# Tracing the four sink heads ahead of the query projection, and storing gates 6 to 8 before their sigmoid

## Chip, cores and metric

One core of one Trainium2 chip. The metric is device time in microseconds (us) from launch to the end of the program, as a median over runs. A core has TensorE (PE), VectorE (DVE), ScalarE (ACT), GpSimd (POOL) and SyncE (SP, which here only issues DMAs). Each works through its own list of instructions, and semaphores hold an instruction back until what it needs is there.

## The reference, cut to what matters

Two layers; each is a half-step feed-forward, a mixing block, and another half-step feed-forward. The mixing block projects the normed input once and feeds three kinds of attention, whose outputs are merged under sigmoid gates:

```python
h = rms_norm(x, mix_norm[l])
(nq, nkc, nvc, nks, nvs, nkw, nvw, ngate, sq, sk, sv, wq, wk, wv, bgate) = jnp.split(h @ w_in[l], SPLIT_POINTS, axis=-1)
y_nsa = nsa_attention(...)            # 8 heads, queries nq, RMS-normed per head
y_sb  = stick_breaking_attention(...) # 4 heads
y_swa = swa_sink_attention(...)       # 4 heads, window 128, a sink logit in the softmax
g = sigmoid(bgate).reshape(B, S, 3, D_MODEL)
merged = g[:, :, 0] * (y_nsa @ w_up_nsa[l]) + g[:, :, 1] * (y_sb @ w_up_sb[l]) + g[:, :, 2] * (y_swa @ w_up_swa[l])
x = x + merged @ w_out[l]
```

The sequence has 512 positions, D_MODEL is 1024, a head is 64 wide. All is float32; the kernel forms a float32 product as three matmuls of a high and a low part.

## The kernel before, in words

Positions lie in four tiles of 128 (`NT`), the model width in eight tiles (`KD`). The order of instructions on each engine is made when the program is built: the code is traced in the order in which it is written, each tile takes a buffer of its pool in that order, and a scheduler then places each instruction on its engine's list when its own model of the engines says that it can start. So the code's order decides who gets a buffer first, and the scheduler decides who stands before whom.

PSUM has eight banks, each of them one buffer (`b0` to `b7`). `psum(...)` says which banks the tiles of a name take in turn. The next tile of a bank can't be written before the last reader of the one before it.

`mix_front` makes everything that comes ahead of the 8 NSA heads: six projections (`project`, L670), head norms, transposes, the stick-breaking heads, the compressed keys and values, and the four heads with sinks (`sliding`). Between them it computes gates ahead. There are 24 gate tiles (3 branches by 8 columns). Gates 0 to 8 (`EARLY = 9`) come by `gate_early` in `mix_front`: 24 matmuls each (L204 to L206, output `g`, weights split by `pieces` into `ghi` on ACT at L195 and `glo` on DVE at L196), a multiplication on DVE (L1092), a sigmoid on ACT (L1075) and a store to DRAM (`gkept`, L1076). Gates 9 to 23 are computed while the NSA heads run and get their sigmoid in `mix_back` (L1201).

One head of `sliding` takes four score tiles (L863, two matmuls of 128x256 each, output `s`), reads each of them on DVE with the bias added and the row's bound found (L865), takes the exponential on ACT (`exp`, L816), divides on POOL (L876), transposes (L879 to L887) and multiplies by the values. `exp` puts each exponential behind all sigmoids traced up to there (`behind`, an order on ACT without a semaphore), so that ACT changes its table once, at the first exponential.

Before the change the end of `mix_front` runs: compressed keys and values; `project(l, 5)`, the queries of NSA; gate 6; `evacuate` (L689) and `head_norms` of the queries (L701 and L702 the sums, L351 to L356 the root, L707 the scaling on DVE, L709 the weights on POOL); their transposes; gates 7 and 8; then `sliding` with score banks 0 and 1. The gates have banks 6 and 2.

Of the kernel before, what the change touches and what calls it, by code (L numbers as in the profile page):

```python
# [12 lines left out]
AF = mybir.ActivationFunctionType  # L13
# [38 lines left out]

EARLY = 9
MORE = (2, 1, 1, 1, 1, 1, 2)

COMPRESS = ((), (0, 1), (2,), (3,))

# [37 lines left out]
def trunk(ctx, tc, I, out):  # L95
    nc = tc.nc
    pe, act, dve, pool, sp = nc.tensor, nc.scalar, nc.vector, nc.gpsimd, nc.sync
# [9 lines left out]
    def nm(s):  # L107
        cnt[0] += 1
        return f"{s}_{cnt[0]}"
# [19 lines left out]
    def psum(**sets):  # L129

        turn.clear()
        for tag, ids in sets.items():
            turn[tag] = itertools.cycle(ids)

    def bank(tag):
        i = next(turn[tag])
        return ps.tile([P, S], F32, name=nm(tag), tag=f"b{i}")
# [541 lines left out]
    def heads(ap, n):  # L679
        return ap.rearrange("p (h d) -> p h d", h=n)  # L680
# [129 lines left out]
    sigmoids = {}  # L810
# [131 lines left out]
    def compress_out(l, p, which):  # L942

        pre = unit("cp")[0:DH]
        act.copy(pre, p[0:DH, 0:CW])
        dve.tensor_tensor(pre, pre, p[DH:P, 0:CW], op=ALU.add)
        hid = unit("cp")[0:DH]
        sigmoids[which] = act.activation(hid, pre, AF.Sigmoid)
        dve.tensor_tensor(hid, hid, pre, op=ALU.mult)
        pb = bank("f")  # L950
        for c in range(2):
            pe.transpose(pb[:, c * DH : (c + 1) * DH], hid[:, c * P : (c + 1) * P], ident[0:DH, 0:DH])
        hT = unit("cp")[:, 0:P]
        dve.tensor_copy(hT, pb[:, 0:P])
        w2 = sm.tile([P, 2, DH], F32, name=nm("w2"), tag="w2", bufs=1)
        sp.dma_start(w2, I[f"w2{which}"][l])
        p = bank("f")
        for g in range(2):
            for c in range(2):
                pe.matmul(p[0:32, g * DH : (g + 1) * DH], hT[:, c * DH + g * 32 : c * DH + g * 32 + 32], w2[:, c], start=c == 0, stop=c == 1)  # L960
        return p[0:32, 0:P]
# [26 lines left out]
    def compressed_v(p):  # L988
        vc = sm.tile([64, 2, 2, DH], F32R, name=nm("vc"), tag="vc", bufs=1)
        for r in (0, 32):  # L990
            act.copy(vc[r : r + 32, :, 0], heads(p, 2))
        for r in (0, 32):
            dve.tensor_tensor(vc[r : r + 32, :, 1], heads(p, 2), f32(vc[0:32, :, 0]), op=ALU.subtract)
        return vc
# [77 lines left out]

    def gate_early(l, i, nrm, between=lambda: None):
        g = gate_logits(l, i, nrm, "gs", between)
        sigmoids["early"] = act.activation(g, g, AF.Sigmoid)  # L1075
        sp.dma_start(gkept[i], g)  # L1076

    def gate_logits(l, i, nrm, tag, between=lambda: None):
# [35 lines left out]
    def mix_front(l, nrm, more):  # L1114
        rows = sm.tile([P, 6, DH], F32, name=nm("rows"), tag="rows", bufs=1)
        sp.dma_start(rows, I["hnorms"][l : l + 1].rearrange("a b c -> a (b c)").to_broadcast([P, 6 * DH]).rearrange("p (b c) -> p b c", b=6))
        sinks = sm.tile([P, 2 * SWH], F32, name=nm("sinks"), tag="sinks", bufs=1)
        sp.dma_start(sinks[:, 0:SWH], I["sinks"][l : l + 1].to_broadcast([P, SWH]))
        dve.tensor_scalar(sinks[:, SWH:], sinks[:, 0:SWH], -1.0, None, ALU.mult)

        for i in (0, 2):
            dve.scalar_tensor_tensor(rows[:, 4 + i // 2], rows[:, i], 0.125, rows[:, i + 1], ALU.mult, ALU.mult)
        psum(acc=(4, 5, 0, 1), f=(7, 2, 3), g=(6,))
        b = project(l, 0, nrm)
        nrm.means()
        rc = nrm.col
        more(1, nrm.spread)
        raw = evacuate(b, 0, 512, rc)
        sq = transposed([r[:, 0:256] for r in raw], SBH, False, "u")
        sk = transposed([r[:, 256:512] for r in raw], SBH, True, "u")  # L1130
        more(MORE[0] - 1)
        psum(acc=(4, 5, 0, 1), f=(7,), s=(2,), t=(3,), o=(6,))
        b = project(l, 1, nrm)
        sv = v_prepare(b, 0, SBH, rc, "u")
        raw = evacuate(b, 256, 256, rc, "gl")
        sb = stick_breaking(sq, sk, sv)
        next(sb)
        blks = [blocks(l, [r[:, i * P : (i + 1) * P] for r in raw], which) for i, which in enumerate("kv")]
        more(MORE[1])
        b = project(l, 2, nrm)  # L1140
        y_sb = [next(sb)]
        raw = evacuate(b, 0, 256, rc)
        gates = sm.tile([P, NT, 3 * NH], F32, name=nm("gates"), tag="gates", bufs=1)
        for t in range(NT):
            sigmoids["gates"] = act.activation(gates[:, t], b[t][:, 256:280], AF.Sigmoid, scale=rc[:, t : t + 1])  # L1145
        dve.tensor_tensor(gates[:, 0, 0:NH], gates[:, 0, 0:NH], valid, op=ALU.mult)
        next(sb)
        head_norms(raw, SWH, rows[:, 5])
        more(MORE[2])
        psum(acc=(4, 5), g=(0, 1), f=(7,), s=(2,), t=(3,), o=(6,))  # L1150
        b = project(l, 3, nrm)
        more(MORE[3])
        next(sb)
        raw_k = evacuate(b, 0, 128, rc)
        wv = v_prepare(b, 128, 2, rc, "gl")
        next(sb)
        wq = transposed(raw, SWH, False, "gl")
        raw = raw_k
        y_sb.append(next(sb))
        head_norms(raw, 2)  # L1160
        next(sb)
        wk = transposed(raw, 2, True, "yn")
        psum(acc=(4, 5, 0, 1), f=(7,), t=(3,), o=(6,), c=(2,))
        p = bank("c")
        b = project(l, 4, nrm, lambda g: [compress_in(l, c, blks, p) for c in COMPRESS[g]])
        next(sb)
        psum(acc=(4, 5, 0, 1), f=(3, 7), g=(6,))
        more(MORE[4])
        raw = evacuate(b, 0, 256, rc)
        nv = v_prepare(b, 256, 4, rc, "u")  # L1170
        head_norms(raw, 4)
        nk = transposed([r[:, 0 : 2 * DH] for r in raw], 2, True, "gl", 32)
        nk += transposed([r[:, 2 * DH :] for r in raw], 2, True, "u")
        compressed_k(compress_out(l, p[:, 0:CW], "k"), nk)
        vc = compressed_v(compress_out(l, p[:, CW:], "v"))
        psum(acc=(4, 5, 0, 1), f=(3, 7), g=(6, 2))
        b = project(l, 5, nrm)
        more(MORE[5])
        raw = evacuate(b, 0, 512, rc)
        head_norms(raw, NH, rows[:, 4])  # L1180
        nq = transposed(raw, NH, False, "u")
        more(MORE[6])
        psum(acc=(4, 5), s=(0, 1), t=(2, 3, 6), o=(7,))
        y_sw = []
        for h, y in enumerate(sliding(wq, wk, wv, sinks)):
            if h % 2:
                y_sw.append(y)
        return (nq, nk, nv, vc, gates), y_sb, y_sw

    def mix_back(l, after, gls, y_ns, y_sb, y_sw, before_last):  # L1190

        branches = [(br, k0, [split_y(y) for y in ys]) for br, k0, ys in ((1, 4, y_sb), (2, 6, y_sw), (0, 0, y_ns))]
        merged = []
        for c in range(KD):
            w = load("wup", (l, c), KD, P)
            start = exps["last split"] if c < 3 else marks["split"]
            acc = None
            for br, k0, ys in branches:
                g = gls[c * 3 + br]
                if c * 3 + br >= EARLY:  # L1200
                    behind(act.activation(g, g, AF.Sigmoid), start)  # L1201
                p = bank("acc")
                for k, y in enumerate(ys):
                    mm3(p, (w[0][:, k0 + k], w[1][:, k0 + k]), y, k == 0, k == len(ys) - 1)
                dve.tensor_tensor(g, g, p, op=ALU.mult)
                if acc is None:
                    acc = g
                else:
                    pool.tensor_tensor(acc, acc, g, op=ALU.add)
            hi, lo = unit("u", F32R), unit("u", F32R)  # L1210
            act.copy(hi, acc)
            dve.tensor_tensor(lo, acc, f32(hi), op=ALU.subtract)
            merged.append((hi, lo))
        for d in range(KD):
            bring_back(d)
            p = bank("acc")
            w = load("wout", (l, d), KD, P)
            for k in range(KD):
                mm3(p, (w[0][:, k], w[1][:, k]), merged[k], k == 0, k == KD - 1)
            if d == KD - 1:  # L1220
                before_last()
            dve.tensor_tensor(x[d], p, x[d], op=ALU.add)
            after(d)
# [28 lines left out]
    nrm = Crossed(0)  # L1252
    psum(acc=(3, 7, 6, 5), seed=(1,), f=(2,))
    for l in range(L):
# [7 lines left out]
        nrm, nxt = nxt, Crossed(3 * l + 2)  # L1262
# [8 lines left out]
        nrm = nxt  # L1271
        if l + 1 < L:
            nxt = Crossed(3 * (l + 1))
            ffn(l, 2, nrm, nxt.add, lambda: start(l + 1, 1, nxt))
            nrm = nxt
# [67 lines left out]
```

## Time and profile before

| | |
|---|---|
| median of 3 runs | 2374.8 us (2373.76 to 2378.49) |
| time of the profiled execution | 2375.91 us |
| its span, first to last instruction | 2374.1 us |
| mean granted clock of TensorE | 0.991 of full |
| PE, DVE, ACT, POOL busy | 98%, 71%, 50%, 20% of the span |
| mixing block of layer 0, front part and NSA heads | about 390 to 780 us of the span |
| the same of layer 1 | about 1565 to 1955 us |

PE is busy nearly all of the time, so the time follows PE's list: its matmuls, its idle time, and the stretches in which it ran at its lower clock level (1.2 instead of 2.4 GHz). The profiled execution is 1.1 us above the median.

### The profile page before, as it was taken

How to read it: one execution, taken by the hardware profiler on the slowest of the kernel's cores; microseconds unless marked ns; L12 is line 12 of the kernel's file. 1: busy time of each engine (PE TensorE's matmuls, PEld its weight loads, DVE VectorE, ACT ScalarE, POOL GpSimd, SP SyncE). 2: the span in 40 equal slices, each digit the busy share in tenths (PEclk: the TensorE clock that was granted, in tenths of full speed). 3: DMA queues.
4: the chain of work that ended last, by engine and by line, in shares of the span. 5: the costliest groups of instructions: out<-in, count | busy, mean ns of one | idle time of the engine just before them, and what ended most of it. 6: DMA issues, size and time to landing. Idle time of an engine off the chain costs nothing.

```text
span 2374.1 us, 37951 instructions
## 1 busy us (share of the span) xinstructions
PE 2332.0 (98%) x14484; PEld 2068.2 (87%) x14484; DVE 1688.8 (71%) x2979; ACT 1185.3 (50%) x2145; POOL 473.4 (20%) x617
## 2 busy tenths in 40 slices
PE   8999999999999999999999999999999999999999
PEld 8989987877888799899899899888778878998997
DVE  8856864776677798558788568638767777985684
ACT  6533543564666555335445345435556665552351
POOL 2011011522333420110100100114333344101100
PEclk9999999999999999999999999999999999999999
DMA  6544443232323345444344444423323243544433
GB/s 205 149 122 130 132 126 108 82 129 89 95 78 120 117 138 159 124 126 140 113 137 145 129 132 126 142 94 98 120 77 96 78 132 120 141 136 133 142 113 100
DMA packets 95474, 289.24 MB, mean 122 GB/s; under 512 B 11573, under 2 KB 13410, under 8 KB 95292
## 3 DMA queue, kind: packets, MB, share of 16 engines
q1 hardware_dynamic: 89100, 264.28, 34.0%
q0 software_dynamic: 6192, 22.55, 5.8%
q8 instruction: 113, 1.85, 0.3%
q14 instruction: 69, 0.57, 0.1%
HBM read 275.70 MB, written 11.08 MB: 121 GB/s over the span
## 4 chain that ended last, share of the span: by engine, by line
PE 90%; DVE 6%; ACT 2%; issue 1%; DMA 1%; POOL 0%; SPq 0%; ACTq 0%; DVEq 0%; POOLq 0%
PE X L411 20%; PE acc L206 11%; PE acc L204 11%; PE acc L205 11%; PE W L411 10%; PE acc L670 7%; PE Y L411 5%; PE o L778 2%; PE s L761 1%; PE s L762 1%; PE g L204 1%; PE g L206 1%; PE g L205 1%; PE f L736 1%; PE c L937 1%
## 5 line engine op out<-in xcount | busy, mean ns | idle before, releaser
L189 ACT CAST whi<-wraw 128x1024 fp32r<-128x1024 f32 (+4 forms) x224 | 193.1, 867 | 370.1 <-PE acc L205 249.1
L190 DVE TENSOR_TENSOR wlo<-wraw,whi 128x1024 fp32r<-128x1024 f32 (+4 forms) x224 | 241.0, 1080 | 180.7 <-ACT whi L189 180.4
L411 ACT CAST whi<-u 128x1024 fp32r<-128x1024 f32 x156 | 163.8, 1050 | 252.4 <-DVE u L411 161.3
L206 PE MATMUL acc<-u,wlo 128*128 128x512 f32 x704 | 275.9, 395 | 1.8 <-DVE wlo L190 1.8
L204 PE MATMUL acc<-u,whi 128*128 128x512 f32 x704 | 276.7, 395 | 0.0
L205 PE MATMUL acc<-u,whi 128*128 128x512 f32 x704 | 276.3, 394 | 0.0
L411 DVE TENSOR_TENSOR wlo<-u,whi 128x1024 fp32r<-128x1024 f32 x164 | 204.6, 1247 | 23.1 <-ACT whi L411 22.6
L670 PE MATMUL acc<-whi,u 128*128 128x512 f32 (+2 forms) x768 | 219.5, 363 | 0.0
L435 POOL DMA_DIRECT2D u<-in_wgu x43 | 37.6, 875 | 755.4 <-DMA u<-in_wgu 430.4
L411 PE MATMUL X<-u,whi 128*128 128x256 f32 x1376 | 180.6, 284 | 5.0 <-ACT Y L411 3.8
L411 PEld LDWEIGHTS X<-u,whi 128*128 128x128 f32 x1376 | 171.0, 189 | 8.5 <-ACT Y L411 4.2
L206 PEld LDWEIGHTS acc<-u,wlo 128*128 128x128 f32 x704 | 132.4, 188 | 33.5 <-DVE wlo L190 2.6
L204 PEld LDWEIGHTS acc<-u,whi 128*128 128x128 f32 x704 | 132.5, 188 | 31.4 <-ACT whi L189 0.8
L205 PEld LDWEIGHTS acc<-u,whi 128*128 128x128 f32 x704 | 132.5, 188 | 30.3
L670 PEld LDWEIGHTS acc<-whi,u 128*128 128x128 f32 x768 | 136.5, 188 | 23.6 <-issue 1.7
L670 PE MATMUL acc<-wlo,u 128*128 128x512 f32 (+2 forms) x384 | 138.5, 361 | 1.1 <-DVE wlo L190 1.1
L196 DVE TENSOR_TENSOR glo<-wraw,ghi 128x256 fp32r<-128x256 f32 x192 | 86.8, 454 | 61.7 <-ACT ghi L195 57.1
L195 ACT CAST ghi<-wraw 128x256 fp32r<-128x256 f32 x192 | 76.8, 404 | 107.1 <-PE g L205 50.5
L236 POOL TENSOR_TENSOR ssum<-ssum,e 128x512 f32<-128x512 f32 x42 | 61.4, 1461 | 314.2 <-ACT e L235 303.3
L646 DVE SCALAR_TENSOR_TENSOR e<-acc,rrow 128x512 f32<-128x512 f32 x64 | 44.2, 690 | 108.2 <-PE acc L206 108.2
L204 PE MATMUL acc<-u,ghi 128*128 128x512 f32 x272 | 113.1, 416 | 0.7 <-ACT gates L1145 0.6
L206 PE MATMUL acc<-u,glo 128*128 128x512 f32 x272 | 110.2, 409 | 0.0
(329 smaller groups left out, 5798.5 us busy)
## 6 DMA issues: line engine op xcount, KB each, us to landing
wraw<-in_wgu SPq DMA_DIRECT2D x104, 512.0 KB, 4.2
tt<-in_wgu SPq DMA_DIRECT2D x68, 512.0 KB, 4.4
wraw<-in_wd SPq DMA_DIRECT2D x64, 384.0 KB, 3.1
wraw<-in_wbg SPq DMA_DIRECT2D x48, 512.0 KB, 3.7
u<-in_wgu SPq DMA_DIRECT2D x43, 512.0 KB, 4.8
u<-in_wgu POOLq DMA_DIRECT2D x43, 512.0 KB, 5.5
wraw<-in_wd SPq DMA_DIRECT2D x64, 320.0 KB, 3.2
wraw<-in_wup SPq DMA_DIRECT2D x16, 512.0 KB, 3.7
```

The lines of the kernel that those rows point to most:

```text
L189: marks["split"] = act.copy(hi, raw)
L190: dve.tensor_tensor(lo, raw, f32(hi), op=ALU.subtract)
L195: act.copy(hi, raw)
L196: dve.tensor_tensor(lo, raw, f32(hi), op=ALU.subtract)
L204: pe.matmul(o, w[0], a[0], start=start, stop=False)
L205: pe.matmul(o, w[0], a[1], start=False, stop=False)
L206: pe.matmul(o, w[1], a[0], start=False, stop=stop)
L236: pool.tensor_tensor(self.sum, self.sum, sq, op=ALU.add)
L411: return lambda *a, **kw: tc.keep_in_program_order(getattr(self.engine, op)(*a, **kw))
L646: dve.scalar_tensor_tensor(e, p, 0.5, nrm.row, ALU.mult, ALU.mult)
L670: pe.matmul(o, a, b[:, j], start=k + m + t % per == 0, stop=True, skip_group_check=True)
L778: pe.matmul(o[:, q0 : q0 + n], v[kb], a[:, c0 : c0 + n], start=start and i == 0, stop=True, skip_group_check=True)
```

## The change

In `mix_front` the four sink heads are now traced right after the compressed values, ahead of `project(l, 5)`, and their banks are other ones: scores in 2 and 6, transposes in 3, outputs in 7. The gates that follow still have banks 6 and 2, in this order. Gates 6, 7 and 8 (`TAKEN = 6`) are stored before their sigmoid, which they now get in `mix_back` as gates 9 to 23 do.

```diff
 EARLY = 9
 MORE = (2, 1, 1, 1, 1, 1, 2)
+
+TAKEN = 6
...
     def gate_early(l, i, nrm, between=lambda: None):
         g = gate_logits(l, i, nrm, "gs", between)
-        sigmoids["early"] = act.activation(g, g, AF.Sigmoid)
+        if i < TAKEN:
+            sigmoids["early"] = act.activation(g, g, AF.Sigmoid)
         sp.dma_start(gkept[i], g)
...
         vc = compressed_v(compress_out(l, p[:, CW:], "v"))
+        psum(acc=(4, 5, 0, 1), s=(2, 6), t=(3,), o=(7,))
+        y_sw = []
+        for h, y in enumerate(sliding(wq, wk, wv, sinks)):
+            if h % 2:
+                y_sw.append(y)
+        b = project(l, 5, nrm)
         psum(acc=(4, 5, 0, 1), f=(3, 7), g=(6, 2))
-        b = project(l, 5, nrm)
         more(MORE[5])
         raw = evacuate(b, 0, 512, rc)
         head_norms(raw, NH, rows[:, 4])
         nq = transposed(raw, NH, False, "u")
         more(MORE[6])
         psum(acc=(4, 5), s=(0, 1), t=(2, 3, 6), o=(7,))
-        y_sw = []
-        for h, y in enumerate(sliding(wq, wk, wv, sinks)):
-            if h % 2:
-                y_sw.append(y)
         return (nq, nk, nv, vc, gates), y_sb, y_sw
...
                 g = gls[c * 3 + br]
-                if c * 3 + br >= EARLY:
+                if c * 3 + br >= TAKEN:
                     behind(act.activation(g, g, AF.Sigmoid), start)
```

What it does to the lists shows at three places, all in layer 0. Lines of the changed kernel are 2 higher up to `gate_early` and 3 or 4 higher behind it.

PE, between the third and the fourth sink head's scores (`s`), before. `g` is a gate, here gate 7, `f_5739` a transpose of the compressed values:

```order
L863 MATMUL s_6294<-yn_5222,gl_5068 128x256
L863 MATMUL s_6294<-yn_5229,gl_5068 128x256
L863 MATMUL s_6299<-yn_5222,gl_5068 128x256
L863 MATMUL s_6299<-yn_5229,gl_5068 128x256
L952 MATMUL f_5739<-tri,cp_5736 128x64 x2
L204 MATMUL g_6047<-u_3607,ghi_6070 128x512
L205 MATMUL g_6047<-u_3607,ghi_6070 128x512
L206 MATMUL g_6047<-u_3607,glo_6071 128x512
L204 MATMUL g_6047<-u_3660,ghi_6070 128x512
L205 MATMUL g_6047<-u_3660,ghi_6070 128x512
L206 MATMUL g_6047<-u_3660,glo_6071 128x512
```

PE, from the last scores of the fourth head on, in the changed kernel. `t` are transposes of the first head's probabilities, `o` its output, and `g_6154` is gate 6:

```order
L881 MATMUL t_5796<-tri,e_985_5765 128x128
L882 MATMUL t_5796<-tri,e_987_5770 128x128
L883 MATMUL t_5796<-tri,e_987_5770 128x128
L884 MATMUL t_5796<-tri,e_989_5775 128x128
L865 MATMUL s_5982<-yn_5222,gl_5075 128x256
L865 MATMUL s_5982<-yn_5229,gl_5075 128x256
L780 MATMUL o_5795<-pt_5801,gl_4982 128x256
L887 MATMUL t_5805<-tri,e_991_5780 128x128
L888 MATMUL t_5805<-tri,e_989_5775 128x128
L889 MATMUL t_5805<-tri,e_991_5780 128x128
L780 MATMUL o_5795<-pt_5802,gl_4982 128x256
L206 MATMUL g_6154<-u_3396,ghi_6157 128x512
```

Where 24 matmuls of gate 7 stood between scores, all 32 score matmuls of the four heads now stand ahead of the first matmul of any of the gates 6 to 8. The queries' projection (`acc`, L670) has not moved on PE: it stands ahead of nearly all scores in both lists.

DVE, around the scaling of the queries by their norms (`rw`), before. `glo` are pieces of gate weights, `vc` the compressed values, `e_1124` the first score tile of the fourth head:

```order
L356 SCALAR_TENSOR_TENSOR hr_5936<-rs_a_5951,hr_5936 128x32
L707 TENSOR_TENSOR rw_5927<-rw_5927,hr_5936 128x512
L707 TENSOR_TENSOR rw_5928<-rw_5928,hr_5936 128x512
L707 TENSOR_TENSOR rw_5929<-rw_5929,hr_5936 128x512
L707 TENSOR_TENSOR rw_5930<-rw_5930,hr_5936 128x512
L196 TENSOR_TENSOR glo_6128<-wraw_6095,ghi_6127 128x256
L993 TENSOR_TENSOR vc_5751<-f_5746,vc_5751 32x2x64 x2
L196 TENSOR_TENSOR glo_7727<-wraw_7724,ghi_7726 128x256
L1092 TENSOR_TENSOR gs_6137<-g_6094,rrow_4000 128x512
L196 TENSOR_TENSOR glo_7737<-wraw_7724,ghi_7736 128x256
L196 TENSOR_TENSOR glo_7747<-wraw_7724,ghi_7746 128x256
L865 ISA e_1124_6355,neg_6349<-s_6352,tt_6347 128x128
```

DVE, right behind the same scaling in the changed kernel; `e_1043` to `e_1049` are the score tiles of the fourth head, `pt` a low part of transposed probabilities:

```order
L871 TENSOR_SCALAR sk_5898<-neg_5896,sinks_3800 128x4
L867 ISA e_1043_5970,neg_5964<-s_5967,tt_5962 128x128
L867 ISA neg_5964 128x1
L995 TENSOR_TENSOR vc_5751<-f_5746,vc_5751 32x2x64 x2
L875 TENSOR_TENSOR den_5897<-den_5897,sk_5898 128x4
L876 RECIPROCAL den_5897<-den_5897 128x4
L867 ISA e_1045_5975,neg_5964<-s_5972,tt_5962 128x256
L867 ISA neg_5964 128x1
L775 TENSOR_TENSOR pt_5802<-t_5796,pt_5801 128x512
L867 ISA e_1047_5980,neg_5964<-s_5977,tt_5962 128x256
L867 ISA neg_5964 128x1
L867 ISA e_1049_5985,neg_5964<-s_5982,tt_5962 128x256
```

The four scalings stood behind twelve of the sixteen score tiles and among the gates' pieces. They now stand behind twelve score tiles and ahead of the last four with no piece of a gate between them.

ACT, in `mix_back`, where the last NSA output (`yn`) is split and the fourth set of `w_up` weights (`whi_8563`) is cast, before:

```order
L801 COPY yn_7396<-o_7562 64x512
L806 CAST u_8435<-yn_7396 128x512
L189 CAST whi_8563<-wraw_8561 128x1024
L1201 ACT_TABLE_LOAD
L1201 ACTIVATE rw_7811<-rw_7811 128x512
L1201 ACTIVATE rw_7856<-rw_7856 128x512
L1201 ACTIVATE rw_7766<-rw_7766 128x512
```

ACT, the same place in the changed kernel; `u_8405` and `u_8408` hold gates 6 to 8:

```order
L808 CAST u_8432<-yn_7393 128x512
L1205 ACT_TABLE_LOAD
L1205 ACTIVATE u_8408<-u_8408 128x512 x2
L1205 ACTIVATE u_8405<-u_8405 128x512
L191 CAST whi_8563<-wraw_8561 128x1024
L1205 ACTIVATE rw_7808<-rw_7808 128x512
L1205 ACTIVATE rw_7853<-rw_7853 128x512
L1205 ACTIVATE rw_7763<-rw_7763 128x512
```

The table's load and three sigmoids moved ahead of that cast.

## Rows read from the trace of the kernel before

**Rows 1.** The page: busy time, share of the span and instructions by engine.

```profile
PE 2332.0 (98%) x14484; PEld 2068.2 (87%) x14484; DVE 1688.8 (71%) x2979; ACT 1185.3 (50%) x2145; POOL 473.4 (20%) x617
```

**Rows 2.** Windows: stretch and its length, busy PE, PEld, DVE, ACT, POOL, granted clock, DMA.

```profile
552.87:583.20 30.33, 29.29 (x156) 22.66 (x154) 24.86 (x87) 14.82 (x38) 6.24 (x7) 1.00 0.27 90
557.10:582.50 25.40, 24.70 (x137) 19.26 (x136) 20.72 (x81) 11.71 (x31) 3.06 (x2) 1.00 0.30 97
582.40:604.00 21.60, 17.81 (x69) 13.04 (x69) 10.74 (x31) 13.70 (x45) 12.78 (x22) 0.76 0.23 71
604.00:755.00 151.00, 150.85 (x840) 127.00 (x839) 116.85 (x352) 102.34 (x278) 53.71 (x116) 1.00 0.33 108
1735.00:1760.40 25.40, 24.69 (x137) 19.28 (x136) 20.61 (x81) 11.75 (x31) 3.00 (x2) 1.00 0.31 95
1760.40:1782.00 21.60, 17.48 (x81) 12.84 (x80) 11.97 (x30) 16.19 (x54) 15.41 (x25) 0.92 0.25 81
```

**Rows 3.** Groups by line, PE, 557.1 to 582.5 us.

```profile
L204 PE MATMUL g<-u,ghi 128*128 128x512 f32 x23 | 9.7, 421 | 0.1
L205 PE MATMUL g<-u,ghi 128*128 128x512 f32 x23 | 9.2, 401 | 0.0
L206 PE MATMUL g<-u,glo 128*128 128x512 f32 x22 | 8.8, 401 | 0.0
```

**Rows 4.** Timeline of PE: start, length, operation, idle before and its releaser.

```profile
567.11 0.74 PE L863 MATMUL s<-yn,gl 128*128 128x256 f32 x4
568.13 0.85 PE L863 MATMUL s<-yn,gl 128*128 128x256 f32 x4 [0.29 <-DVE neg L865]
...
575.02 0.40 PE L204 MATMUL g<-u,ghi 128*128 128x512 f32 x1
575.25 0.40 PE L205 MATMUL g<-u,ghi 128*128 128x512 f32 x1
...
584.74 0.65 PE L206 MATMUL g<-u,glo 128*128 128x512 f32 x1 [1.87 <-DVE glo L196]
...
587.74 0.63 PE L206 MATMUL acc<-u,glo 128*128 128x512 f32 x1
```

**Rows 5.** Groups by line and shape, DVE, 552.87 to 583.2 us.

```profile
L865 DVE CUSTOM_DVE_ANT_0 e<-s,tt 128x256 f32<-128x256 f32 x9 | 3.6, 417 | 0.6 <-PE s L863 0.6
L689 DVE TENSOR_SCALAR rw<-acc,rcol 128x512 f32<-128x512 f32 x4 | 3.0, 750 | 1.4 <-PE acc L670 1.2
L1092 DVE TENSOR_TENSOR gs<-g,rrow 128x512 f32<-128x512 f32 x2 | 1.4, 692 | 0.7 <-PE g L206 0.7
```

**Rows 6.** Timelines of DVE and POOL around the scaling of the queries.

```profile
578.61 4.67 DVE L707 TENSOR_TENSOR rw<-rw,hr 128x512 f32<-128x512 f32 x4
583.20 1.48 DVE L196 TENSOR_TENSOR glo<-wraw,ghi 128x256 fp32r<-128x256 f32 x1
585.20 0.42 DVE L196 TENSOR_TENSOR glo<-wraw,ghi 128x256 fp32r<-128x256 f32 x1
...
579.44 4.95 POOL L709 TENSOR_TENSOR rw<-rw,rows 128x512 f32<-128x512 f32 x3 [24.09 <-DVE rw L707]
595.81 3.85 POOL L876 TENSOR_SCALAR e<-e,den 128x128 f32<-128x128 f32 x8 [0.33 <-DVE den L874]
```

**Rows 7.** Timeline of ACT: before the first exponential, and in `mix_back`.

```profile
588.29 0.63 ACT L1075 ACTIVATE gs<-gs 128x512 f32<-128x512 f32 x1
588.94 1.28 ACT L816 ACT_TABLE_LOAD   x1
...
774.55 1.05 ACT L189 CAST whi<-wraw 128x1024 fp32r<-128x1024 f32 x1 [3.85 <-PE acc L205]
776.91 1.67 ACT L1201 ACTIVATE rw<-rw 128x512 f32<-128x512 f32 x3
```

**Rows 8.** Timeline of PE at the last NSA head, layer 0.

```profile
761.09 0.49 PE L1064 MATMUL o<-pt,vc 64*128 64x512 f32 x1 [1.43 <-DVE pt L1063]
```

## The prediction

> **What bounds the kernel now.** I read the page first: PE is busy for 98% of the span [rows 1], so a change pays only through PE's idle time and through stretches at its lower clock level. Next I cut the mixing block into windows and looked for both. In the 151 us from 604 to 755 us, the NSA heads, PE is busy for 150.85 us at full clock: the gates 9 to 23 fill every wait, and nothing can be won there. In the window just before, 582.4 to 604.0 us, it is busy for 17.81 of 21.6 us and the granted clock is 0.76; in layer 1 the same place has 17.48 of 21.6 us and 0.92 [rows 2]. These two windows are what there is to win. Their cause shows on ACT: the first exponential of the sink heads waits until gate 8's sigmoid (588.29 us) and a table load (1.28 us) are over [rows 7], though the scores of three heads were read long before. PE runs out of gate pieces in the meantime, since DVE has four scalings of 4.67 us in front of them [rows 6], and stands for 1.87 us [rows 4].
>
> What these windows cost. Layer 0: 21.6 − 17.81 = 3.8 us idle. Clock 0.76 between a full level of 1 and a half of 0.5 means 0.48 x 21.6 = 10.4 us at the half level. At full, gate matmuls start 0.23 us apart (575.02, 575.25); after the stall eight of them stand from 584.74 to 587.74 us, 3.00 / 7 = 0.43 apart [rows 4]. So work at the half level loses 46% of its time. Taking some 2 us of the 10.4 as idle, 8.4 x 0.46 = 3.8 us. Together 7.6. Layer 1: 4.1 us idle and 0.16 x 21.6 = 3.5 us at the half level, of which I take 1.3 as idle: 2.2 x 0.46 = 1.0. Together 5.1.
>
> **The change part by part.** *The projection* stays where it is: PE's list still has it ahead of nearly all scores. Nothing is won or lost by it.
>
> *The gates 6 to 8* are what moves. Before, PE ran 23 + 23 + 22 = 68 of their 72 matmuls between 557.1 and 582.5 us, woven between the sink heads' scores [rows 3]. Now gate 6 has bank 6, which the sixteenth score tile holds last, and on PE's list all 32 score matmuls stand ahead of it. So its start is the time at which DVE has read the last score tile. DVE is in order too, and has the whole of the queries' norms among those reads. I take the time from DVE's work from 552.87 us on, when it takes the first tile of the queries' projection; up to there the lists are the same. In the window to 583.20 DVE is busy for 24.86 us [rows 2]. Off go nine pieces of gates at 0.34 from start to start (0.42 long [rows 6], and operations overlap by some 0.08; the tenth begins where the window ends) and two multiplications of a gate by the row at 0.61 (0.69 long [rows 5]): 3.1 + 1.2 = 4.3. On come four more score tiles (0.42 long [rows 5], three at 0.35 and a half one at 0.22: 1.3), three pairs of sum and reciprocal of 128x4 (estimate, as other tiny operations: 0.37 a pair, 1.1), the low part of the compressed values (about 0.6) and one of 128x512 (0.61, as the multiplication): 3.6. That leaves 24.1 us of work. It also waits: 5.5 us in that window before; bounds are 0.7 (what it still waits for the projection, about half of the 1.4 in [rows 5]) and 5.5. In the new list each score waits for one of two banks, and the sums of squares for ACT; I take 3.0, the middle. Gate 6 then starts at 552.87 + 24.1 + 3.0 = 580.0 us.
>
> What lag that is: at 580.0 us PE still owes 68 x 0.23 = 15.8 us of gates, and is ahead by four score matmuls, seven transposes and two products of the first head (an estimate from their sizes, 1.5 us). It stands where it stood at 582.5 us only at 580.0 + 15.8 − 1.5 = 594.3 us: **11.8 us late**. It is idle for as long: the window of 25.4 us held 24.70 of work [rows 2], so without the gates and with the 1.5 us PE has 10.4 us of work for 22.9 us, and the 0.7 us that it idled before is the difference.
>
> *What it pays behind the hole.* PE comes out of a longer pause than the one of 1.87 us, after which eight matmuls ran at 0.43 [rows 4]: 8 x 0.2 = 1.6 us. ACT has three casts of queries that wait for POOL's weights (1.65 us each [rows 6]) ahead of the fourth head's exponentials, and DVE's next gate pieces stand behind that head's sums: about 1 us more. I take 2.5.
>
> *What it wins.* The windows of 7.6 and 5.1 us go: by 580 us the exponentials of three heads are done, since their ACT table no longer waits for gate 8, and gates 6 to 8 then stand between the transposes and products of the sink heads. And at the last head PE waits 1.43 us [rows 8], once in each layer; its list now has nine matmuls of `w_up` (2.1 us) there, so I take this as won, 1.4 a layer.
>
> *Sigmoids.* Three per layer move to `mix_back`, 1.67 us for three, with the table load of 1.28 us, ahead of a cast that before waited 3.85 us for a buffer [rows 7]. 1.67 + 1.28 = 2.9 < 3.85: nothing. Without that cover it would be up to 2.9 us a layer. The stores of these gates move behind other loads on SP; the next gate's weights are issued behind a bias table that waits for the fourth head's scores, at 580 us, but they need a buffer that gate 6 still holds: nothing.
>
> **Sum.** Layer 0: 11.8 + 2.5 − 7.6 − 1.4 = +5.3. Layer 1: its window before is the same (24.69 of 25.4 [rows 2]), so 11.8 + 2.5 − 5.1 − 1.4 = +7.8. Together **+13 us**. The profiled execution took 2375.9 us, 1.1 above the median: 2389 on its scale, **2388 us** on that of the median.
>
> **The rivals.**
>
> *A longer hole.* While POOL's three weightings ran (579.44 on), DVE's four scalings took 4.67 us, and the piece behind them 1.48 instead of 0.42 [rows 6]: the two slow each other. In the new list POOL also has eight divisions of the first two heads (3.85 us for eight [rows 6]) ahead of the weightings, beside DVE's last reads. If that costs DVE 2 us more, if it waits the full 5.5 us, and the stalls behind the hole come back by half (3 us), it is 2 + 2.5 + 3 = 7.5 us a layer more, 2403 us. The Trainium skill (SBUF — State Buffer, Who interferes with whom) has the mechanism: a DVE instruction with two inputs in SBUF contends with a GpSimd one that reads SBUF, and whoever comes second is fully blocked. By this rule the scalings and the pieces block, as 1.48 against 0.42 shows, and the reads of scores, with one input in PSUM, don't; so it speaks for a hole little longer than mine.
>
> *Paid back: no change.* The two layers gain 7.6 + 5.1 + 2.8 = 15.5 us and lose twice the lag and 2.5. If DVE hardly waits (0.7 instead of 3.0) and PE comes out of the hole at full clock, the loss is 2 x 9.5 = 19, so +3.5, 2378 us. Against it: the half level follows the shorter pause before.
>
> *Faster.* If DVE's list gave way and the scores ran at their own pace, two tiles in 1.02 us (567.11 to 568.13 us, where the next two begin [rows 4]), sixteen would take 8.2 us, less than the 10.4 us of work that PE has; no hole, and 15.5 us won: 2359 us. It decides where twice (lag + 2.5) is 15.5, a lag of 5.3 us, gate 6 at 573.5 us. DVE's work alone ends at 552.87 + 24.1 = 577.0 us, which is what speaks against it.
>
> **How the numbers follow.** About 0.2% (4.7 us) is what a measurement of this kernel can tell from no change. Forecast (2380 to 2396): 0.68. Longer hole: 0.16. Paid back: 0.10. Faster: 0.06. The forecast's own bounds are ±2.3 us of waiting a layer and ±2 us of what comes behind. The range runs from the paid-back case to the longer hole, 2378 to 2404 us. Slower takes the forecast, nearly all of the longer hole and little of the rest, 0.83; same 0.11, faster 0.06.
>
> **What would show it.** In the changed trace, layer 0: PE's idle time between 557 and 580 us near 12 us, released by DVE's reads of scores (L867 there), with the first matmul of gate 6 right behind the last of them; the granted clock below 1 in that stretch or just behind it; the first exponential near 566 us; the window of gates 6 to 8 behind it with PE full; the same in layer 1. The 1.43 us at the last head gone. The prediction is wrong if gate 6 starts before 574 us, or if PE is as idle behind the hole as it was.

## The result

The changed kernel takes **2390.43 us** (median of 4 runs, 2388.93 to 2392.32), the kernel before took 2376.24 us beside it (4 runs, 2373.76 to 2378.49). The ratio is 1.0062, with a 95% interval of 1.005 to 1.0074: 14.2 us slower. The forecast was 2388 us, +13 us.

The profiled execution of the changed kernel took 2388.93 us. Its page answers to [rows 1]: PE is busy for 6.8 us more with the same 14484 instructions, although the program has no more work, and the span is 13.0 us longer (2387.1 against 2374.1).

```profile
PE 2338.8 (98%) x14484; PEld 2072.8 (87%) x14484; DVE 1693.8 (71%) x2979; ACT 1188.2 (50%) x2145; POOL 479.7 (20%) x617
```

The mean granted clock is 0.986 of full, before 0.991, so part of the longer busy time is the same matmuls at the lower level. The windows show where. Their columns are those of [rows 2]; the changed kernel's stretch starts 1.3 us earlier, since its first reading of the queries' projection begins at 551.56 us and not at 552.87.

```profile
557.00:581.65 24.65, 15.81 (x69) 11.35 (x70) 17.70 (x86) 14.79 (x50) 11.23 (x14) 0.60 0.14 36
581.65:603.65 22.00, 22.00 (x107) 18.51 (x108) 12.68 (x28) 10.45 (x28) 6.70 (x19) 0.91 0.36 115
...
604.00:755.00 151.00, 150.30 (x817) 124.94 (x816) 111.06 (x332) 96.90 (x260) 52.19 (x101) 1.00 0.29 95
...
1735.00:1760.00 25.00, 18.72 (x94) 14.27 (x93) 19.36 (x84) 14.62 (x47) 7.37 (x11) 0.73 0.17 53
```

In layer 0 PE was busy for 24.70 of 25.4 us ahead of 582.5 us [rows 2]; now it is busy for 15.81 of 24.65 us, at 0.60 of the clock. Behind it, where it had stood for 3.8 us, it is now full. A hole of the same kind is in layer 1 (18.72 of 25.0 us, 0.73), though its list is no copy of layer 0's: gate 5's matmuls still run there up to 1738 us, behind the first reading of the projection (1729.27 us), and gate 6 begins at 1765.39 us.

PE's timeline in the hole, layer 0, has what each wait was for:

```profile
561.51 0.54 PE L865 MATMUL s<-yn,gl 128*128 128x256 f32 x2 [1.61 <-DVE cp L948]
...
567.65 1.43 PE L865 MATMUL s<-yn,gl 128*128 128x256 f32 x4 [1.48 <-DVE neg L867]
...
575.13 0.79 PE L865 MATMUL s<-yn,gl 128*128 128x256 f32 x2 [2.17 <-DVE neg L867]
575.72 0.44 PE L881 MATMUL t<-tri,e 128*128 128x128 f32 x1
...
579.20 0.58 PE L780 MATMUL o<-pt,gl 128*128 128x256 f32 x1 [1.19 <-ACT pt L774]
...
581.65 0.80 PE L206 MATMUL g<-u,ghi 128*128 128x512 f32 x1 [0.55 <-DVE neg L867]
...
585.23 0.63 PE L208 MATMUL g<-u,glo 128*128 128x512 f32 x1
585.66 0.44 PE L206 MATMUL g<-u,ghi 128*128 128x512 f32 x1
...
586.86 0.27 PE L881 MATMUL t<-tri,e 128*128 128x128 f32 x1
```

The reader sees gate 6 begin at 581.65 us, released by DVE's last reads of scores, and nine gate matmuls some 0.43 us apart before they come at full clock (585.66). PE's own small work is stretched too: a transpose (L881) of 128x128 takes 0.44 us in the hole and 0.27 us behind it.

On DVE, ACT and POOL, in the same stretch:

```profile
567.16 0.43 DVE L867 CUSTOM_DVE_ANT_0 e<-s,tt 128x256 f32<-128x256 f32 x1 [1.42 <-DMA tt<-rows_d]
...
572.01 2.58 DVE L709 TENSOR_TENSOR rw<-rw,hr 128x512 f32<-128x512 f32 x4
...
576.73 0.42 DVE L867 CUSTOM_DVE_ANT_0 e<-s,tt 128x256 f32<-128x256 f32 x1 [0.74 <-PE t L883]
...
579.17 0.69 DVE L775 TENSOR_TENSOR pt<-t,pt 128x512 fp32r<-128x512 f32 x1 [2.02 <-ACT pt L774]
580.82 0.42 DVE L867 CUSTOM_DVE_ANT_0 e<-s,tt 128x256 f32<-128x256 f32 x1 [0.95 <-PE t L888]
...
581.17 0.42 DVE L867 CUSTOM_DVE_ANT_0 e<-s,tt 128x256 f32<-128x256 f32 x1
...
564.74 0.40 ACT L818 ACTIVATE e<-e,neg 128x128 f32<-128x128 f32 x1 [1.53 <-DVE rs_a L357]
...
577.03 0.40 ACT L729 CAST st<-rw 128x256 fp32r<-128x256 f32 x1 [1.91 <-POOL rw L711]
...
572.15 3.61 POOL L878 TENSOR_SCALAR e<-e,den 128x128 f32<-128x128 f32 x4 [0.81 <-DVE neg L870]
575.73 4.94 POOL L711 TENSOR_TENSOR rw<-rw,rows 128x512 f32<-128x512 f32 x4
```

The first exponential stands at 564.74 us (before, its table's load alone began at 588.94 [rows 7]). The third head's bias table comes late (1.42 us). The four scalings take 2.58 us and not 4.67 [rows 6], and POOL's weightings now come behind them; POOL's divisions of one head beside them take 3.61 us, those of the head before 1.73 (569.61 us).

Two of the fourth head's reads wait for something that the prediction doesn't have. The kernel keeps three buffers of each of the tiles `e1` to `e3` (`BUFS`), so the fourth head's tiles lie where the first head's lay, and its reads at 576.73 and 580.82 us, which write them, wait for the first head's transposes (L883, L888). So gate 6 stands behind the first head's whole chain: its exponentials, its divisions on POOL and its transposes.

**The two layers.** The last NSA output of a layer (ACT, `yn`, at 768.74 and 1944.47 us before) stands here at:

```profile
773.92 0.58 ACT L803 COPY yn<-o 64x512 f32<-64x512 f32 x1 [3.36 <-PE o L780]
...
1957.52 0.58 ACT L803 COPY yn<-o 64x512 f32<-64x512 f32 x1 [3.37 <-PE o L780]
```

From the first reading of the projection (552.87 and 551.56 us) to the first of them it is 215.9 us before and 222.4 after: **+6.5 in layer 0** (forecast +5.3). From the one to the other it is 1175.7 and 1183.6: **+7.9 in layer 1** (forecast +7.8), this with the last part of layer 0 in it.

### The profile page after: what moved, and what is told of

The parts are those of the page before. It is cut to its first block, busy times and chain, and to the rows that moved or that the text cites. A ratio compares the mean times of both kernels' runs of the same rounds, so it can differ in the third digit from the quotient of the medians.

```text
span 2387.1 us, 37945 instructions
## 1 busy us (share of the span) xinstructions
PE 2338.8 (98%) x14484; PEld 2072.8 (87%) x14484; DVE 1693.8 (71%) x2979; ACT 1188.2 (50%) x2145; POOL 479.7 (20%) x617
## 4 chain that ended last, share of the span: by engine, by line
PE 89%; DVE 6%; issue 2%; ACT 1%; DMA 1%; POOL 1%; SPq 0%; DVEq 0%; ACTq 0%; POOLq 0%
PE X L413 20%; PE acc L208 11%; PE acc L206 11%; PE acc L207 11%; PE W L413 10%; PE acc L672 8%; PE Y L413 5%; PE o L780 2%; PE g L206 1%; PE g L207 1%; PE g L208 1%; PE s L763 1%; PE s L764 1%; PE f L738 1%; PE c L939 1%
```

## The experiments

The theory was: the loss is the time in which PE has no gate between the sink heads' scores. The rivals: the moved sigmoids; contention between DVE and POOL (one slowing the other where they run side by side); a load that comes late; the banks alone. All ratios are to the kernel before, timed beside it on the same chip (2374.87, 2375.42, 2375.04 and 2376.98 us in the four groups). One pair of windows serves for all: 557 to 640 us and 1735 to 1820 us, from ahead of the heads into the NSA heads. The kernel before:

```profile
557.00:640.00 83.00, 78.51 (x414) 63.32 (x413) 56.87 (x191) 51.41 (x149) 27.14 (x47) 0.94 0.29 91
1735.00:1820.00 85.00, 80.17 (x433) 64.64 (x432) 59.78 (x198) 54.34 (x157) 30.51 (x54) 0.98 0.27 86
```

and the changed kernel, 8.8 and 8.4 us idle and at 0.86:

```profile
557.00:640.00 83.00, 74.16 (x378) 60.29 (x379) 52.92 (x184) 47.95 (x140) 27.81 (x50) 0.86 0.27 85
1735.00:1820.00 85.00, 76.64 (x390) 62.10 (x389) 54.56 (x178) 48.87 (x140) 28.51 (x50) 0.86 0.24 80
```

**The two parts alone.** The order of the heads, with the banks that came with it, and no sigmoid moved:

```diff
-TAKEN = 6
+TAKEN = 9
```

> The changed kernel with the other part alone: the sink heads are traced ahead of the projection of the queries, and gates 6 to 8 keep their early sigmoid. If the hole in PE's list makes the loss, this is as slow as the change, 2388 to 2392 us, with gate 6 near 581.6 us in layer 0; the sigmoids in the last part are worth 1 us at most (0.5 a layer at its first low part). If the sigmoids that were moved carry the loss, it comes back to 2376 us or less.

Measured: 2390.41 us, ratio 1.0062 (1.0049 to 1.0074), the same as the whole change. Gate 6 starts 30.2 us behind the first reading of the projection, in the changed kernel 30.1. The order of the heads, with its banks, carries the whole loss.

The sigmoids alone, on the kernel before (a gate kept from 6 on gets its sigmoid in `mix_back`, the heads stay behind the queries):

```diff
-        sigmoids["early"] = act.activation(g, g, AF.Sigmoid)
+        if i < TAKEN:
+            sigmoids["early"] = act.activation(g, g, AF.Sigmoid)
```

> The kernel before with one part of the change alone: gates 6 to 8 are stored before their sigmoid, and the sink heads stay where they were. If the stall of before in 582 to 604 us comes from the exponentials that wait for gate 8's sigmoid, the first exponential of the sink heads moves from 590 us to about 566 us, the PE wait of 1.87 us and the half clock behind it go, and most of 7.6 + 5.1 us is won, less about 1 us for the sigmoids in the last part: about 2366 us. If the stall comes from DVE's four scalings of 4.67 us that stand ahead of the gate pieces, it stays: 2374 to 2378 us. If the sigmoids in the last part are what the change loses by, it is slower than before: 2380 us or more.

Measured: 2369.99 us, ratio 0.9977 (0.9967 to 0.9987): faster, by 4.9 us and not by the 9 expected. Its windows:

```profile
557.00:640.00 83.00, 78.50 (x430) 62.89 (x429) 60.45 (x201) 51.92 (x153) 31.70 (x54) 1.00 0.27 91
1735.00:1820.00 85.00, 80.87 (x437) 66.40 (x437) 60.72 (x201) 51.31 (x153) 30.91 (x54) 0.96 0.27 92
```

In layer 0 PE idles just as long (4.5 us), but in shorter pieces, and the clock stays at 1. The first exponential moved to 571.05 us. In the profiled execution layer 0 takes 211.7 us from the first reading of the projection to the last NSA output, 4.2 less than before. So the late exponentials made one long stall and the half clock behind it, not the idle time itself. Layer 1 won nothing by it (1177.3 us from output to output, before 1175.7). There a stall of 3.10 us stands, and its rows on PE, DVE and POOL name another cause:

```profile
1760.53 0.80 PE L864 MATMUL s<-yn,gl 128*128 128x256 f32 x2 [3.10 <-DVE neg L866]
...
1754.34 4.65 DVE L708 TENSOR_TENSOR rw<-rw,hr 128x512 f32<-128x512 f32 x4
...
1755.12 1.66 POOL L710 TENSOR_TENSOR rw<-rw,rows 128x512 f32<-128x512 f32 x1 [2.22 <-DVE rw L708]
...
1757.02 3.09 POOL L710 TENSOR_TENSOR rw<-rw,rows 128x512 f32<-128x512 f32 x2
```

The score waits for a read that stands behind the four scalings, and these run beside POOL's weightings (4.65 us; 2.72 in layer 0 of this kernel, where the weightings come behind them).

**Is it the banks?** If gates 6 to 8 don't share banks with the scores, nothing keeps them out of the hole. First with one bank for each:

```diff
-        psum(acc=(4, 5, 0, 1), s=(2, 6), t=(3,), o=(7,))
+        psum(acc=(4, 5, 0, 1), s=(2,), t=(3,), o=(7,))
...
-        psum(acc=(4, 5, 0, 1), f=(3, 7), g=(6, 2))
+        psum(acc=(4, 5, 0, 1), f=(3, 7), g=(6,))
```

> The changed kernel with its banks alone changed: the scores of the sink heads have bank 2 only, and gates 6 to 8 have bank 6 only, so that no gate waits for a score tile. If the shared banks make the hole, the gates run between the scores again: PE is full from 557 to 581 us, the clock stays at 1, and the two layers get back their 14 us or more: 2362 to 2376 us. If DVE's order or its contention with POOL holds PE whatever the banks, PE stands about as long as in the changed kernel and the time stays above 2385 us.

Measured: 2395.63 us, ratio 1.0087 (1.0073 to 1.01). The hole at 557 to 581 us is gone (PE busy for 23.21 of 24 us at full clock), as the first forecast said, and still the time is that of the second: a new hole of 7.0 us stands in 604 to 640 us. With two banks for each:

```diff
-        psum(acc=(4, 5, 0, 1), f=(3, 7), g=(6, 2))
+        psum(acc=(4, 5, 0, 1), f=(3, 7), g=(0, 1))
```

> The changed kernel with gates 6 to 8 in banks 0 and 1 (free once the queries are read from them) and the scores in banks 2 and 6 as in the change, so two banks for each. If the shared banks alone make the loss, the gates lie between the scores, the heads run as early as in the changed kernel, and nothing is left of the hole: 2362 to 2370 us. If what decides is that gates are taken as soon as they can start, so that the heads' last transposes and products stand alone wherever the gates run out, the window 557 to 581 us is full and PE idles 5 us or more behind it, as with one bank each (7.0 us in 604 to 640): 2384 to 2398 us.

Measured: 2383.59 us, ratio 1.0035 (1.0023 to 1.0048), just below the second forecast and, by the profile, of its kind:

```profile
557.00:640.00 83.00, 75.56 (x396) 60.07 (x396) 54.35 (x182) 47.93 (x141) 28.98 (x47) 0.96 0.28 91
1735.00:1820.00 85.00, 79.52 (x408) 63.74 (x407) 56.17 (x183) 49.43 (x144) 31.09 (x49) 0.92 0.27 89
```

Ahead of 581 us PE is full (23.80 of 24 us). Its gates go on to 604.68 us, and the next comes at 622.69 us; in between are the last heads' transposes and products, each behind its own chain:

```profile
604.68 0.40 PE L208 MATMUL acc<-u,glo 128*128 128x512 f32 x1
...
607.27 0.35 PE L780 MATMUL o<-pt,gl 128*128 128x256 f32 x1 [1.05 <-DVE y L804]
607.91 0.33 PE L887 MATMUL t<-tri,e 128*128 128x128 f32 x1 [0.28 <-DVE pt L775]
609.07 0.39 PE L894 MATMUL o<-pt,gl 128*128 128x256 f32 x1 [0.49 <-ACT pt L774]
...
622.69 0.50 PE L206 MATMUL acc<-u,ghi 128*128 128x512 f32 x1 [0.40 <-DVE rw L1095]
```

This kernel placed six gates there (6 to 8, and three of those that fill the NSA heads). To take the banks away altogether and leave only three gates:

```diff
-EARLY = 9
-MORE = (2, 1, 1, 1, 1, 1, 2)
+EARLY = 6
+MORE = (2, 1, 1, 1, 1, 0, 0)
```

> The changed kernel with six gates computed ahead instead of nine, so that gates 6 to 8 are the first of those that fill the NSA heads and have banks 4 and 5, which no score uses. The program then has room for three gates ahead of the NSA heads, as in the changed kernel, and puts all three between the scores. If the shared banks make the loss, it is gone: 2362 to 2372 us. If the loss is that the heads stand alone on PE wherever no gate is left, the window 557 to 581 us is full, the hole lies behind it, in the transposes and products, and with three gates where the kernel with banks 0 and 1 had six it is longer than there (7.2 us idle): 9 to 14 us idle in layer 0, 2385 to 2400 us.

Measured: 2414.0 us, ratio 1.0156 (1.0142 to 1.017), slower than either theory said:

```profile
557.00:640.00 83.00, 70.15 (x352) 56.35 (x351) 53.70 (x182) 47.24 (x139) 30.75 (x54) 0.84 0.19 63
1735.00:1820.00 85.00, 73.19 (x343) 58.12 (x343) 48.13 (x152) 42.16 (x123) 28.58 (x47) 0.80 0.15 50
```

PE is full ahead of 581 us (23.64 of 24) and then idles for 12.5 us up to 640, within the 9 to 14 expected. What the forecast lacked is the clock: 0.84 and 0.80, and 0.62 in 581 to 604 us. Here no gate shares a bank with a score, and as few gates as in the changed kernel run ahead of the NSA heads (72 matmuls), yet it is some 22 us slower (1.0156 against 1.0062). So the shared banks are not the root of the loss: they fix where the gates stand. By these two kernels, behind the scores, between transposes and products, is the better of the two places, but the place is not all that differs: the longest wait here, 3.91 us at 585.49 us, is a score behind the four scalings, which take 4.84 us (2.58 in the changed kernel).

Two things no run settles. All kernels with the heads ahead have one bank for transposes, the kernel before has three, and the second set of a head's transposes waits until the first is read (0.28 us at 607.91 us above, up to 1.03 us in the kernel with three gates). And no kernel has a fourth buffer for `e1` to `e3`, or more gates than nine in the new order.

**How much is DVE's list, and how much contention?** Without the queries' head norms (the kernel leaves them out, so this part isn't computed):

```diff
-        head_norms(raw, NH, rows[:, 4])
```

> The changed kernel without the norms of the eight NSA heads' queries (their squares, sums, root, scalings and weights are left out, so this part isn't computed). If gate 6 starts when DVE's list has read the last score tile, the four sums, the root and the four scalings that leave that list (about 6 us with their waits) let it start about 6 us earlier, near 575 us in layer 0, and the time falls by about that in each layer: 2376 to 2382 us. If the hole is set by PE's or ACT's side of the heads and not by DVE's list, gate 6 stays within 2 us of 581.6 and the time within 4 us of the changed kernel's.

Measured: 2386.62 us, ratio 1.0046 (1.0034 to 1.0059). Gate 6 starts 27.8 us behind the first reading instead of 30.1: 2.3 us earlier, not 6, and the time is 3.8 us below that of the order alone, 1.9 a layer. That is the second forecast (gate 6 at 580.47 us, the time within 4 us): other engines hold the hole more than DVE's list does. DVE has 2.3 us less to do in 557 to 581 us (14.82 against 17.09) and waits elsewhere instead, 1.16 and 0.95 us of it for the first head's transposes. The bias tables of all four heads loaded ahead into one buffer:

```diff
+        tabs = whole("tt")
         for h in range(SWH):
...
-            tab = unit("tt")[:, 0:SWW]
+            tab = tabs[:, h * SWW : (h + 1) * SWW]
```

> The changed kernel with the four bias tables of the sink heads loaded ahead into one buffer, so that the third head's read doesn't wait for its table (1.42 us on DVE, 1.48 us on PE in layer 0). If the chain from score to score sets the hole, gate 6 starts about 1.4 us earlier and the time falls by 1 to 3 us over both layers: 2387 to 2389 us. If the wait is only passed on to the next one (DVE's scalings, ACT's casts behind POOL's weights), the time stays within 1 us of the changed kernel's.

Measured: 2388.23 us, ratio 1.0057 (1.0044 to 1.007). Gate 6 starts 1.3 us earlier (28.8 us behind the first reading), as the chain says; the gain of some 1 us lies inside the interval. With this and POOL's weightings taken away, the weights being folded into the reading from PSUM and the squares taken from there:

```diff
-            dve.tensor_scalar(v, banks[t][:, c0 : c0 + width], rcol[:, t : t + 1], None, ALU.mult)
+            w = wrow.unsqueeze(1).to_broadcast([P, NH, DH])
+            dve.scalar_tensor_tensor(heads(v, NH), heads(o, NH), rcol[:, t : t + 1], w, ALU.mult, ALU.mult)
...
+                act.activation(sq, src[t][:, 0:width], AF.Square, scale=rcol[:, t : t + 1])
```

> The changed kernel with both reliefs: the weights of the queries' norm folded into their reading from PSUM (no POOL weightings) and the bias tables loaded ahead. If what costs the change its time is that no gate stands between the scores, these reliefs shorten the hole by what they take out of the chain (ACT's casts behind POOL's weights and one table wait, about 4 us of waits a layer, half of it on the chain) and it stays slower than before: 2379 to 2386 us. If contention of DVE and POOL and the load on DVE are what makes the change slow, they bring it to 2375 us or below, as near to 2366.62 us as the same edits bring the kernel with the heads in their old place.

Measured: 2386.23 us, ratio 1.0042 (1.0029 to 1.0055). Gate 6 stands 28.4 us behind the first reading. The reliefs bring back some 4 us of the loss, and the kernel is still 11 us slower than before, as the first forecast had it (by a hair above its 2386 us): contention and a late table are a small part of it. In all these kernels the fourth head's last reads still wait for the first head's transposes, 0.95 us in each.

**A faster one.** The same fold on the kernel with the sigmoids alone:

> The kernel before with gates 6 to 8 stored before their sigmoid (2369.99 us), and besides that the weights of the queries' norm folded into their first reading from PSUM, so that POOL's four weightings beside DVE's four scalings are gone (their squares are taken from PSUM). If POOL's weightings are what stretches the scalings (4.65 us in layer 1, against 2.58 us where POOL's came behind them) and holds ACT's casts, the scalings take about 2.6 us, PE's wait of 3.10 us in layer 1 goes, and 3 to 6 us are won: 2364 to 2367 us. If the scalings are slow by themselves or the waits move on, 2368 us or more.

Measured: 2368.33 us, ratio 0.9969 (0.9956 to 0.9981). The stall of 3.10 us is gone and the scalings take 3.02 us in layer 1, but only some 1.7 us of the 3 to 6 came, less than the intervals tell apart, so the second forecast holds: the waits moved on; in 1784 to 1930 us PE idles 1.3 us more than without the fold (143.95 busy against 145.23). With the tables ahead as well:

> As the one with the folded weights, and the four bias tables loaded ahead into one buffer. In the kernel with the sigmoids alone the table wait was 0.38 us on DVE, so this is worth 0 to 1 us: the same as without it, or up to 1 us faster. More than 1.5 us slower would say that the longer hold of one table buffer delays the first tables of the NSA heads.

Measured: **2366.62 us**, ratio 0.9963 (0.9951 to 0.9976), the fastest here, some 24 us below the changed kernel; the step from the one without the tables is within the intervals. With a tenth gate computed ahead:

```diff
-EARLY = 9
-MORE = (2, 1, 1, 1, 1, 1, 2)
+EARLY = 10
+MORE = (2, 1, 1, 1, 1, 1, 3)
```

> The fastest kernel so far (sigmoids later, weights folded, tables ahead; 2366.62 us) with one gate more computed ahead of the NSA heads (ten instead of nine), behind the queries' transposes. If PE's waits in the sink heads are a lack of matmuls to put between, its 24 matmuls fill some of the 4.3 us that it stands in layer 0 between 557 and 604 us and of the 3.4 us in layer 1, and the NSA heads with one gate less stay full: 2361 to 2365 us. If the gates that are there are enough and the waits stand in PE's list whatever is behind them, or if the NSA heads then run short, 2366 us or more.

Measured: 2371.38 us, ratio 0.9982 (0.9973 to 0.9991): the second forecast, and nothing won. In 557 to 640 us PE idles as long as without it (3.4 us against 3.3), in layer 1 1.2 us less; the time grew all the same, though the two intervals still touch. Where it went isn't settled: of the 3.1 us between the two spans, some 2 lie behind the last NSA output of layer 1.

## Why the prediction was right, point by point

**The sum** came out (+13 against +14.2), the sign and its size for the reason given: gates 6 to 8 leave PE's list between the scores and PE idles at half clock until they come. The order alone costs as much as the whole. That the sum came so close is in part luck: by the terms below the lag is 3 us a layer longer than forecast, what is paid behind the hole 0.7 us less, and 1.1 us in layer 0 and 2.2 us in layer 1 that no term holds take back the rest.

**The start of gate 6** was forecast at 27.1 us behind the first reading (580.0 − 552.87) and is 30.1 us. The term that was mis-sized is the waits: "I take 3.0, the middle" of 0.7 and 5.5 us. DVE is busy for 22.39 of the 30.44 us from 551.56 to 582.00 us; so its work is about 22 (forecast 24.1) and its waits 8:

```profile
551.56:582.00 30.44, 21.52 (x100) 16.02 (x99) 22.39 (x93) 18.04 (x57) 14.06 (x19) 0.67 0.14 39
```

The largest waits are for a cast that ACT runs behind its wait for POOL's weightings (2.02 us), for the table (1.42 us) and for the first head's transposes (0.95 and 0.74 us). The rule behind it, "the time at which DVE has read the last score tile", holds to the row in layer 0; in layer 1 gate 6 starts 1.2 us behind the last read, after a product of the first head that waits 1.28 us for ACT. And what bounds that time is only partly DVE's list, as the kernel without the norms shows: the first head's whole chain over ACT, POOL, DVE and PE lies in front of the last reads, by the three buffers of `e1` to `e3`. The chain of waits of the changed kernel in 557 to 583 us, by line:

```profile
by line: DMA tt<-rows_d 11.0%; DVE e L867 9.7%; POOL rw L711 9.5%; issue 9.1%; POOL e L878 8.6%; ACT u L740 5.6%; ACT ssum L703 4.1%; PE g L206 3.1%; DVE rs_a L356 2.8%; PE s L865 2.8%; DVE pt L775 2.7%; DVE ss L704 2.6%; DVE hr L358 2.5%; 
```

Four engines and a DMA share it, and no single line has more than an eighth. POOL's divisions and weightings together have 18%: from 572.15 to 578.25 us the chain runs through POOL alone, then through ACT's cast, the first head's transposed probabilities and its second transposes to the last two reads.

**"PE's idle time near 12 us"** is 8.8: the lag is longer, but the small matmuls fill more of it at the half level. (The 15.8 us of gates that PE owes are 68 x 0.23 = 15.6, which changes nothing.) That the clock also falls inside the hole (0.60) and not only behind it was in the text as "in that stretch or just behind it" and in no term of the sum.

**What it pays behind the hole** (2.5 us): nine matmuls at 0.43 where eight were forecast, 9 x 0.2 = 1.8 (in layer 1 eleven), and no second stall.

**What it wins.** The 1.43 us at the last head [rows 8] is gone in both layers of the changed kernel, so that term is right. It stands in the one with gates in banks 0 and 1 (1.44 and 1.43), so the heads' order alone doesn't remove it; with the sigmoids alone it stands in layer 0 (1.43) and not in layer 1. The windows of 7.6 and 5.1 us went too, but the explanation beside them holds by half: it blamed the exponentials' wait for gate 8's sigmoid, and lifting that alone gave back 4.9 us of 12.7. With the later start and 1.8 us behind, layer 0 would sum to 14.8 + 1.8 − 7.6 − 1.4 = 7.6 us against 6.5 measured, and layer 1, if it were as late, to 14.8 + 1.8 − 5.1 − 1.4 = 10.1 against 7.9; the 1.1 and 2.2 us are not assigned.

**Sigmoids: "nothing".** Nearly. The table's load and three sigmoids stand where forecast, but the low part that the next matmul needs comes later, and PE waits 1.39 us there (0.88 before):

```profile
775.89 1.28 ACT L1205 ACT_TABLE_LOAD   x1
777.18 1.68 ACT L1205 ACTIVATE u<-u 128x512 f32<-128x512 f32 x3
...
784.15 0.50 PE L208 MATMUL acc<-u,wlo 128*128 128x512 f32 x1 [1.39 <-DVE wlo L192]
```

That is 0.5 us a layer. Neither part alone does it: the wait is 0.52 us with the sigmoids alone and 0.74 with the order alone.

**The rivals.** *A longer hole* came by half: of its three conditions, DVE's waits went beyond the full 5.5 us, but POOL didn't cost DVE 2 us more, and the stalls behind the hole didn't come back. DVE's scalings got faster and POOL's divisions slower (3.61 against 1.73). The Trainium skill (SBUF — State Buffer, Who interferes with whom) says that of a DVE instruction with two inputs in SBUF and a POOL one that reads SBUF, whoever comes second is blocked: that agrees with POOL being stretched once DVE's two-input scalings ran ahead of it. *Paid back* did not come: it asked for waits of 0.7 us on DVE, and they were above even the upper bound of 5.5. *Faster* rested on the scores running with no hole. The kernels with own banks for the gates show that this would not have sufficed: PE full to 581 us, and still 2383.59 us or more.

## What to carry to other kernels

Here a chain of small dependent steps cost PE next to nothing where big independent matmuls stood between its steps [rows 2], and the stock of these was limited: moving the chain ahead moved it away from them. Ask not only who holds the bank, but how much filler (matmuls that wait for nothing in the chain) is left for the stretch in which the chain now stands, where it runs out, and which buffers tie the chain's end to its start. When two edits come together, price each alone: here one was worth 4.9 us and the other cost three times as much (15.5 us by itself).

## What was not expected of the hardware

- The same idle time went with two clocks: 4.5 us of idle in layer 0's window stood beside a granted clock of 0.94 in the kernel before (with a pause of 1.87 us [rows 4]) and 1.00 in the one with late sigmoids, whose longest pause there is 1.00 us.
- Four scalings on DVE of 128x512 took 4.65 us beside POOL's weightings and 2.5 to 3.0 us where these were gone or came later; POOL's four divisions took 3.61 us beside the scalings and 1.73 us without.
